# FFN up and gate of a hybrid decoder layer: from feature-major 256-column matmuls to token-major 512-column matmuls, turned back through VectorE and DRAM

## The chip, the cores and the metric

The kernel runs on one core of one Trainium2 chip. A core has a matrix engine (TensorE, PE in the profile, with its weight loads shown as PEld), three engines for elementwise work (VectorE or DVE, ScalarE or ACT, GpSimd or POOL), a queue engine (SyncE, SP) that issues transfers, and 16 DMA engines that carry them. The metric is the device time of one execution in microseconds, given as the median of several runs. Lower is better.

## The reference

The kernel computes one layer of a decoder for 256 tokens of width 1024, all in float32. The first part (norm, two parallel token mixers, an output projection, a residual) is the same before and after. The second part is a gated FFN with a causal convolution over the tokens:

```python
h = rmsnorm(x, norm2_g[l])
up = causal_dwconv(jnp.einsum('bsd,df->bsf', h, w_up[l]), ffn_conv_w[l], ffn_conv_b[l])
act = jax.nn.gelu(up) * jnp.einsum('bsd,df->bsf', h, w_gate[l])
x = x + jnp.einsum('bsf,fd->bsd', act, w_down[l])
```

The FFN is 2816 wide. The convolution has three taps per feature and runs along the tokens, and its weights and bias belong to the feature. A layout with features on the 128 partitions and tokens in the free dimension (feature-major) therefore has one weight per partition, and a tap is a shift in the free dimension. The down projection wants its 128x128 operand with features on the partitions as well.

## The kernel before

**Number format of the matmuls.** Every weight chunk is loaded as float32 (a tile `raw`, 128x2048, 1 MB), split into a rounded part `hi` and a remainder `lo`, and each product is made of three matmuls in TensorE's float32r format (`mm3`, lines 240 to 243: hi by hi, a remainder by hi, hi by the other remainder). The split is one cast on ScalarE (L223; chunks 39, 42 and 43 on VectorE) and one subtraction on VectorE (L224). There are 3 `raw`, 4 `hi` and 3 `lo` buffers.

**The stream of chunks.** All weights form one list, `stream`, in the order of use: chunks 0 to 37 for the first part, 38 to 41 for the output projection, 42 to 74 for the FFN. `advance(i)` emits the splits up to chunk i, and before the split of chunk j the loads up to chunk j+3, all on SP's queue. A load waits until its `raw` buffer has been split; a split waits until TensorE has used the chunk that held its `hi` or `lo` buffer.

**The first part.** The loop over `UNITS` runs the units in the order given; each is cut in quarters. The table `AFTER` names what is emitted behind each quarter: splits (`s5` is the split of chunk 5), evacuations, convolution, recurrence, attention steps (`S`, `P`, `O` with a head's number), and later the four transposes of the second norm (`n00` to `n11`). Two matmul forms occur. `fm_mm` (L245) has a 128x128 block of the weight as the stationary operand and 256 columns, all tokens, as the moving one; its result is feature-major. `tm_mm` (L432) has 128 tokens of the activation as the stationary operand and 512 weight columns as the moving one; its result is token-major, and two tiles hold the two halves of the tokens. With `split=True` the 512 columns come from two blocks of 256 that lie side by side in the chunk; the units ga, gb, pr and pa use this.

**The FFN before.** It has 11 blocks of 256 features. For each block j: up by `fm_mm` (48 matmuls of 256 columns), `up_post` (norm factor `rbf`, convolution, GELU), gate by `fm_mm` (48 more), `gate_post` (multiply, split), and down of block j-1 by `rows_mm` (24 matmuls of 512 columns into the four accumulators `acc`). In block 0 up and gate take the first half of the inner dimension, then the last transposes (`norm2_t(1, 1)`), then the second half; the norm's factors are then broadcast by four matmuls (`norm2_bcast`, tile `rbfp`). The last down block closes the kernel with eight output stores.

**What sets the order.** The framework takes the emitted order as a priority, not as the order itself. A planner walks through the program with its own costs, and puts on each engine's queue the first instruction by priority that it holds to be ready. The order on each queue is then fixed, and on the chip each engine works its queue in that order and waits where data is not there.

Of the kernel before, what the change touches and what calls it, by code (L numbers as in the profile page):

```python
# [8 lines left out]
F32 = mybir.dt.float32  # L9
# [26 lines left out]
AFTER = {  # L36
    "rx0.0": "stats",
    "rg0.0": "s4",
    "rg0.2": "bcast evac1 s5",
    "rg0.3": "s6",  # L40
    "rg1.1": "evac0 evac2",
    "rg1.2": "evac3",
    "rg1.3": "conv0 decay",
    "rg2.0": "s7",
    "rg2.2": "conv1",
    "rg2.3": "s8 split0",
    "k0.1": "s9",
    "k0.2": "s10",
    "k0.3": "conv2 s11",
    "k1.0": "conv3 split1",  # L50
    "k1.3": "s12",
    "k2.3": "s13",
    "ri0.1": "s14",
    "ri0.2": "krs",
    "q0.0": "gelu1",
    "q0.1": "la0 lb0",
    "q0.2": "s15",
    "q1.0": "lc0",
    "q1.2": "s16",
    "q1.3": "s17",  # L60
    "ri1.0": "s18",
    "ri1.3": "ld0 la1",
    "q2.2": "lb1",
    "q3.1": "Tq0 ks0",
    "q3.2": "s19 ks1",
    "q3.3": "s20 qrs gelu0",
    "v0.2": "Tk0",
    "v0.3": "s21",
    "v2.0": "S0",
    "v2.1": "s22",  # L70
    "v2.2": "s23",
    "v3.1": "Tk1",
    "v3.3": "S1 S2",
    "ga0.2": "s24 P0",
    "ga0.3": "s25 lc1 s26 S3",
    "ga1.1": "P1 O0",
    "ga1.3": "Tq1",
    "ga2.1": "P2",
    "ga2.3": "P3",
    "ga3.0": "s27",  # L80
    "ga3.1": "O1",
    "ga3.2": "S6",
    "ga3.3": "S7 O3",
    "gb0.0": "O2 ya0 S4",
    "gb0.1": "S5",
    "gb0.2": "s28",
    "gb1.0": "P6",
    "gb1.2": "ld1 ya1 s29",
    "gb1.3": "P4",
    "gb2.0": "sa1",  # L90
    "gb2.1": "P7 O4",
    "gb2.2": "s30",
    "gb2.3": "ys1",
    "gb3.1": "ys0",
    "gb3.2": "P5",
    "gb3.3": "O6",
    "pr0.0": "s31 sb0",
    "pr0.1": "s32 O5",
    "pr0.2": "O7",
    "pr0.3": "s33",  # L100
    "pr1.2": "sa0",
    "pr2.2": "s34",
    "pr3.2": "s35",
    "pa0.0": "s36",
    "pa1.0": "s37",
    "pa1.3": "s38",
    "pa2.1": "s39",
    "pa2.3": "sb1",
    "pa3.2": "m0",
    "pa3.3": "m1 s40",  # L110
    "wo.3": "m3 s41",
    "wo.5": "m2",
    "wo.11": "n00",
    "wo.12": "s42 n10",
    "wo.15": "n01 s43",
# [4 lines left out]
def trunk_layer(ctx: ExitStack, tc: tile.TileContext, xT, x, vec, win_fm, win_tm, wri, wpr, wpa,  # L120
# [6 lines left out]
    work = ctx.enter_context(tc.tile_pool(name="work", bufs=2))  # L127
    psA = ctx.enter_context(tc.tile_pool(name="psA", bufs=4, space=PSUM))
# [46 lines left out]
    def add(src):  # L175
        stream.append(src)
        return len(stream) - 1
# [560 lines left out]
    act = {}  # L738

    def up_post(j, ps):  # L740
# [3 lines left out]
        for i in range(2):  # L744
            m = 2 * j + i
            w = lambda k: pv[:, V_FW + 3 * m + k:V_FW + 3 * m + k + 1]
            nc.scalar.activation(c[:, i, :], u[:, i, :], AF.Identity, scale=w(2),  # L747
                                 bias=pv[:, V_FB + m:V_FB + m + 1])
            for k in (1, 0):
                d = 2 - k  # L750
                nc.vector.scalar_tensor_tensor(c[:, i, d:], u[:, i, :S - d], w(k), c[:, i, d:],  # L751
                                               op0=OP.mult, op1=OP.add)
# [119 lines left out]
```

## Time and profile before

| | |
|---|---|
| median of three runs | 448.86 us (447.87 to 449.06) |
| the profiled execution | 447.88 us |
| its span, first to last instruction | 446.0 us |
| TensorE busy | 440.8 us, 99% |
| VectorE busy | 313.8 us, 70% |
| ScalarE busy | 261.5 us, 59% |
| DMA, HBM read / written | 79.78 MB / 1.05 MB |
| first up matmul, last acc matmul start | 254.5 us, 440.6 us |

In the profile's rows the number after the engine is the line in the kernel. "out<-in" are the tiles that an instruction writes and reads, xN is a count, and what follows "<-" in a wait is what ended it. In rows of groups the two numbers after the first bar are the busy time in us and the mean duration of one in ns. In a table by stage each engine has its busy time and, in brackets, how many instructions ran; the last three columns are the granted TensorE clock, the busy share of the DMA engines, and GB/s. In rows of a timeline the first number is the start and the second the duration, in us. In rows of DMA issues the last two numbers are the KB of one transfer and the median us from issue to landing. A busy TensorE is no TensorE at its peak, since matmuls overlap.

### The profile page before, as it was taken

How to read it: one execution, taken by the hardware profiler on the slowest of the kernel's cores; microseconds unless marked ns; L12 is line 12 of the kernel's file. 1: busy time of each engine (PE TensorE's matmuls, PEld its weight loads, DVE VectorE, ACT ScalarE, POOL GpSimd, SP SyncE). 2: the span in 40 equal slices, each digit the busy share in tenths (PEclk: the TensorE clock that was granted, in tenths of full speed). 3: DMA queues.
4: the chain of work that ended last, by engine and by line, in shares of the span. 5: the costliest groups of instructions: out<-in, count | busy, mean ns of one | idle time of the engine just before them, and what ended most of it. 6: DMA issues, size and time to landing. Idle time of an engine off the chain costs nothing.

```text
span 446.0 us, 6672 instructions
## 1 busy us (share of the span) xinstructions
PE 440.8 (99%) x2736; PEld 397.3 (89%) x2736; DVE 313.8 (70%) x462; ACT 261.5 (59%) x319; POOL 1.6 (0%) x9
## 2 busy tenths in 40 slices
PE   8999999999999999999999999999999999999996
PEld 8999988888888888888888899999999999999995
DVE  4688996979999775755677888575576575575553
ACT  4687757999996799733141656454354454454420
POOL 1000000000000000000000000000000000000000
PEclk9999999999999999999999999999999999999999
DMA  7995554645575455445545356545645645545202
GB/s 226 373 340 215 216 191 147 205 173 158 181 228 167 127 181 188 155 132 196 191 175 179 114 191 248 195 143 190 220 140 190 216 157 185 202 173 190 94 1 94
DMA packets 17629, 81.24 MB, mean 182 GB/s; under 512 B 1728, under 2 KB 4160, under 8 KB 10944
## 3 DMA queue, kind: packets, MB, share of 16 engines
q1 hardware_dynamic: 16880, 80.22, 51.9%
q10 hardware_dynamic: 720, 0.61, 0.5%
q8 instruction: 21, 0.34, 0.3%
q14 instruction: 8, 0.07, 0.0%
HBM read 79.78 MB, written 1.05 MB: 181 GB/s over the span
## 4 chain that ended last, share of the span: by engine, by line
PE 91%; ACT 5%; DMA 2%; issue 0%; DVE 0%; SPq 0%; ACTq 0%
PE gt L241 5%; PE gt L243 5%; PE gt L242 5%; PE up L243 5%; PE up L242 5%; PE up L241 5%; PE acc L241 4%; PE acc L242 4%; PE acc L243 4%; DMA raw<-in_win_fm 2%; PE rg L241 2%; PE rg L242 2%; PE rg L243 2%; PE ga L241 2%; PE gb L241 2%; PE pr L241 2%
## 5 line engine op out<-in xcount | busy, mean ns | idle before, releaser
L223 ACT CAST hi<-raw 128x2048 fp32r<-128x2048 f32 (+3 forms) x88 | 138.1, 1579 | 100.9 <-PE up L242 32.5
L224 DVE TENSOR_TENSOR lo<-raw,hi 128x2048 fp32r<-128x2048 f32 (+3 forms) x92 | 171.1, 1870 | 32.3 <-PE acc L242 14.0
L241 PE MATMUL up<-h2h,hi 128*128 128x256 f32 x176 | 49.9, 284 | 0.0
L241 PE MATMUL gt<-h2h,hi 128*128 128x256 f32 x176 | 49.9, 283 | 0.0
L243 PE MATMUL up<-h2h,lo 128*128 128x256 f32 x176 | 49.8, 283 | 0.0
L243 PE MATMUL gt<-h2h,lo 128*128 128x256 f32 x176 | 49.8, 283 | 0.0
L242 PE MATMUL gt<-h2l,hi 128*128 128x256 f32 x176 | 49.8, 283 | 0.0
L242 PE MATMUL up<-h2l,hi 128*128 128x256 f32 x176 | 49.8, 283 | 0.0
L241 PEld LDWEIGHTS up<-h2h,hi 128*128 128x128 f32 x176 | 33.7, 192 | 0.4
L242 PEld LDWEIGHTS up<-h2l,hi 128*128 128x128 f32 x176 | 33.7, 192 | 0.3
L242 PEld LDWEIGHTS gt<-h2l,hi 128*128 128x128 f32 x176 | 33.8, 192 | 0.0
L241 PEld LDWEIGHTS gt<-h2h,hi 128*128 128x128 f32 x176 | 33.8, 192 | 0.0
L243 PEld LDWEIGHTS gt<-h2h,lo 128*128 128x128 f32 x176 | 33.8, 192 | 0.0
L243 PEld LDWEIGHTS up<-h2h,lo 128*128 128x128 f32 x176 | 33.7, 192 | 0.0
L241 PE MATMUL acc<-hi,fa 128*128 128x512 f32 x86 | 33.6, 391 | 0.0
L242 PE MATMUL acc<-lo,fa 128*128 128x512 f32 x86 | 33.6, 390 | 0.0
L243 PE MATMUL acc<-hi,fa 128*128 128x512 f32 x86 | 33.5, 389 | 0.0
L743 DVE TENSOR_TENSOR fuc<-up,rbf 128x512 f32<-128x512 f32 x11 | 7.6, 691 | 33.2 <-PE up L243 33.2
L243 PEld LDWEIGHTS acc<-hi,fa 128*128 128x128 f32 x86 | 16.1, 188 | 3.5
L751 DVE SCALAR_TENSOR_TENSOR fuc<-fuc,pv 128x255 f32<-128x255 f32 (+1 forms) x44 | 18.6, 479 | 0.8 <-ACT fuc L747 0.7
L241 PEld LDWEIGHTS acc<-hi,fa 128*128 128x128 f32 x86 | 16.2, 188 | 3.1
L242 PEld LDWEIGHTS acc<-lo,fa 128*128 128x128 f32 x86 | 16.2, 188 | 2.9
(220 smaller groups left out, 1011.1 us busy)
## 6 DMA issues: line engine op xcount, KB each, us to landing
raw<-in_win_tm SPq DMA_DIRECT2D x12, 1024.0 KB, 4.8
raw<-in_win_fm SPq DMA_DIRECT2D x11, 1024.0 KB, 5.7
raw<-in_wup SPq DMA_DIRECT2D x11, 1024.0 KB, 4.8
raw<-in_wgate SPq DMA_DIRECT2D x11, 1024.0 KB, 4.8
raw<-in_wdown SPq DMA_DIRECT2D x11, 1024.0 KB, 4.8
raw<-in_wpr SPq DMA_DIRECT2D x4, 1024.0 KB, 4.9
raw<-in_wpa SPq DMA_DIRECT2D x4, 1024.0 KB, 4.9
raw<-in_wout SPq DMA_DIRECT2D x4, 1024.0 KB, 4.8
```

What stands on the lines that cost most here:

```text
L223: (nc.vector.tensor_copy if on_dve else nc.scalar.copy)(hi[i][:, s], raw[i][:, s])
L224: nc.vector.tensor_sub(lo[i][:, s], raw[i][:, s], f(hi[i][:, s]))
L241: nc.tensor.matmul(o, ah, bh, start=start, stop=False, skip_group_check=skip)
L242: nc.tensor.matmul(o, ah, bl, start=False, stop=False, skip_group_check=skip)
L243: nc.tensor.matmul(o, al, bh, start=False, stop=stop, skip_group_check=skip)
L743: nc.vector.tensor_mul(u, ps, rbf2)
L751: nc.vector.scalar_tensor_tensor(c[:, i, d:], u[:, i, :S - d], w(k), c[:, i, d:], op0=OP.mult, op1=OP.add)
```

## The change

Blocks 0 to 9 become five pairs of 512 features. For each pair, up and gate are computed token-major by `tm_mm` with `split=True`: per result two PSUM tiles (one per 128 tokens), 48 matmuls of 512 columns. The results are then brought to feature-major without TensorE:

- `turn`: VectorE transposes the 32x32 blocks of each PSUM tile within itself into an SBUF tile of 128x1024 (two instructions). Four DMAs, one per group of 32 partitions, write the blocks to a DRAM tile (128 KB each, runs of 1 KB), ordered so that each row of DRAM holds what one feature-major partition needs.
- `back`: one DMA reads the DRAM tile into SBUF (512 KB, rows of 4 KB). It is emitted later, by the entries `ur` and `gr` of `AFTER`. All five DMAs are on SP's queue.
- `pair_up` (entries `fu`): norm factor by two multiplies, convolution of four 128-feature groups, one GELU of 1024 columns. `pair_gate` (entries `fg`): two multiplies by the gate, and the split into the operands of down.

The order is now: in pair 0 up and gate alternate by halves of the inner dimension, in the others up is followed by gate; behind pair p from p = 2 on come the down blocks of pair p-2. After the last pair follow down of blocks 6 and 7, the last block (feature-major as before), and the remaining downs. The stream has the same 33 chunks in the new order. `AFTER` is written anew for the first part as well, and now goes through the FFN. The tiles of the FFN are kept in 15 fixed buffers (`KEPT`).

The diff, with the moved entries of `AFTER` ahead of the FFN cut to samples:

```diff
--- before.py
+++ after.py
+KEPT = {"ups": 1, "upd": 2, "gts": 1, "gtd": 2, "u": 1, "c": 2, "ah": 3, "al": 3}
...
-    "rx0.0": "stats",
-    "rg0.0": "s4",
-    "rg0.2": "bcast evac1 s5",
+    "rx0.0": "stats s4",
+    "rg0.1": "bcast",
+    "rg0.2": "s5 evac1",
...
-    "ga2.3": "P3",
-    "ga3.0": "s27",
-    "ga3.1": "O1",
-    "ga3.2": "S6",
+    "ga2.3": "s27",
+    "ga3.1": "P3",
+    "ga3.2": "O1 S5 S6",
     "ga3.3": "S7 O3",
...
-    "wo.11": "n00",
-    "wo.12": "s42 n10",
-    "wo.15": "n01 s43",
+    "wo.11": "n10 s42",
+    "wo.12": "n00",
+    "wo.14": "s43",
+    "up00.0": "n01 s44",
+    "up00.1": "n11",
+    "up00.3": "bcast2",
+    "gt00.0": "s45",
+    "up01.0": "s46",
+    "gt01.0": "s47",
+    "gt01.1": "ur0",
+    "up10.1": "s48",
+    "up10.2": "gr0",
+    "up11.1": "s49",
+    "up11.3": "fu0",
+    "gt10.1": "s50",
+    "gt10.2": "ur1",
+    "gt11.1": "s51 fg0",
+    "up20.1": "s52",
+    "up20.2": "gr1",
+    "up20.3": "fu1",
...
+    "dn4.1": "s68",
+    "dn4.2": "gr4",
+    "dn4.3": "fu4",
+    "dn5.1": "s69",
+    "dn6.1": "s70",
+    "dn6.3": "fg4",
+    "dn7.1": "s71",
+    "last.0": "s72",
+    "last.2": "s73",
+    "dn8.1": "s74",
 }
...
+    dram = ctx.enter_context(tc.tile_pool(name="dram", bufs=4, space=bass.MemoryType.DRAM))
...
-    c_up, c_gt, c_dn = [], [], []
-    for j in range(NF):
-        c_up.append(add(wup[j]))
-        c_gt.append(add(wgate[j]))
-        if j >= 1:
-            c_dn.append(add(wdown[j - 1]))
-    c_dn.append(add(wdown[NF - 1]))
+
+    NP = NF // 2
+    c_up, c_gt, c_dn = {}, {}, []
+    for p in range(NP):
+        for c, kh in ((c_up, 0), (c_gt, 0), (c_up, 1), (c_gt, 1)) if p == 0 else (
+                (c_up, 0), (c_up, 1), (c_gt, 0), (c_gt, 1)):
+            c[p, kh] = add(two(wup if c is c_up else wgate, 0, 2 * p + kh))
+
+        if p >= 2:
+            c_dn += [add(wdown[j]) for j in (2 * p - 4, 2 * p - 3)]
+    c_dn += [add(wdown[j]) for j in range(2 * NP - 4, 2 * NP - 2)]
+    c_up[NP], c_gt[NP] = add(wup[NF - 1]), add(wgate[NF - 1])
+    c_dn += [add(wdown[j]) for j in range(NF - 3, NF)]
...
-        ps = bank("rbfp")
+        ps = psA.tile([P, 512], F32, tag="A", name="rbfp")
...
-    acc = {(t, hf): psA.tile([P, 512], F32, tag="A", name=f"acc{t}{hf}") for t in range(2) for hf in range(2)}
-    act = {}
+    acc, act, kept = {}, {}, {}
+    def keep(name, p, dt=F32):
+        n = p % KEPT[name]
+        if (name, n) not in kept:
+            kept[name, n] = half(f"f{name}{n}", dt)
+        return kept[name, n]
+    def turn(kind, p, ps):
+        src, dst = keep(kind + "s", p), keep(kind + "d", p)
+        mid = dram.tile([P, 1024], F32, tag="turn", name=f"{kind}m{p}")
+        v = src.rearrange("p (j t c b) -> p t c j b", j=4, t=2, c=4)
+        for t in range(2):
+            nc.vector.transpose(v[:, t], ps[t].rearrange("p (c j b) -> p c j b", c=4, j=4))
+        m = mid.rearrange("(j a) (i f) -> i a j f", j=4, i=4)
+        for i in range(4):
+            nc.sync.dma_start(m[i], src[32 * i:32 * i + 32, :].rearrange("p (j f) -> p j f", j=4))
+        def back():
+            nc.sync.dma_start(dst, mid)
+        item[f"{kind[0]}r{p}"] = back
+        return dst.rearrange("p (i t c b) -> p t c i b", i=4, t=2, c=4)
+    tok32 = lambda a, t: a.rearrange("p (c t i b) -> p t c i b", t=2, i=4, b=32)[:, t]
+    def conv3(c, u, m):
+        w = lambda k: pv[:, V_FW + 3 * m + k:V_FW + 3 * m + k + 1]
+        nc.scalar.activation(c, u, AF.Identity, scale=w(2), bias=pv[:, V_FB + m:V_FB + m + 1])
+        for k in (1, 0):
+            d = 2 - k
+            nc.vector.scalar_tensor_tensor(c[:, d:], u[:, :S - d], w(k), c[:, d:], op0=OP.mult, op1=OP.add)
+    turned, gated = {}, {}
+    def pair_up(p):
+        d = turned["up", p]
+        u, c = keep("u", p), keep("c", p)
+        rb = rbf.rearrange("p (t i b) -> p t i b", t=2, i=4)
+        for t in range(2):
+            nc.vector.tensor_mul(tok32(u, t), d[:, t], rb[:, t, None].to_broadcast([P, 4, 4, 32]))
+        for i in range(4):
+            conv3(kt(c)[:, i, :], kt(u)[:, i, :], 4 * p + i)
+        nc.scalar.activation(c, c, AF.Gelu_apprx_tanh)
+        gated[p] = c
+    def pair_gate(p):
+        c, d = gated[p], turned["gt", p]
+        for t in range(2):
+            nc.vector.tensor_mul(tok32(c, t), d[:, t], tok32(c, t))
+        ah, al = keep("ah", p, F32R), keep("al", p, F32R)
+        split2(ah, al, c)
+        for i in range(2):
+            act[2 * p + i] = tuple(kt(a[:, i * 512:(i + 1) * 512]) for a in (ah, al))
...
-    for j in range(NF):
-        pu, pg = fm_ps(f"up{j}"), fm_ps(f"gt{j}")
-        if j == 0:
-
-            advance(c_up[0] + AHEAD_S)
-            for half_k in range(2):
-                ks = range(4 * half_k, 4 * half_k + 4)
-                for ps, i in ((pu, c_up[0]), (pg, c_gt[0])):
-                    fm_mm(ps, i, h2h, h2l, ks, True)
-                    if not half_k and ps is pu:
-                        norm2_t(1, 1)
-            norm2_bcast()
-            gate_post(0, up_post(0, pu), pg)
-        else:
-            advance(c_up[j] + AHEAD_S)
-            fm_mm(pu, c_up[j], h2h, h2l)
-            c = up_post(j, pu)
-            advance(c_gt[j] + AHEAD_S)
-            fm_mm(pg, c_gt[j], h2h, h2l)
-            gate_post(j, c, pg)
-            advance(c_dn[j - 1] + AHEAD_S)
-            for t in range(2):
-                for hf in range(2):
-                    down(j - 1, t, hf)
+    for p in range(NP):
+        item[f"fu{p}"] = lambda p=p: pair_up(p)
+        item[f"fg{p}"] = lambda p=p: pair_gate(p)
+    item["n11"] = lambda: norm2_t(1, 1)
+    item["bcast2"] = norm2_bcast
+
+    def pair_half(kind, p, kh):
+        c = (c_up if kind == "up" else c_gt)[p, kh]
+        if not kh:
+            open_ps[kind, p] = [bank(f"{kind}{p}{t}") for t in range(2)]
+        advance(c)
+        for k4 in range(4):
+            tm_mm(open_ps[kind, p], c, 4 * kh + k4, k4, h2h, h2l, True)
+            if kh and k4 == 3:
+                turned[kind, p] = turn(kind, p, open_ps[kind, p])
+            yield
+
+    def downs(j):
+        advance(c_dn[j])
+        for t in range(2):
+            for hf in range(2):
+                if j == 0:
+                    acc[t, hf] = psA.tile([P, 512], F32, tag="A", name=f"acc{t}{hf}")
+                down(j, t, hf)
+                yield
+
+    def last_block():
+        pu, pg = fm_ps("upl"), fm_ps("gtl")
+        for ps, i in ((pu, c_up[NP]), (pg, c_gt[NP])):
+            advance(i)
+            for j in range(2):
+                for h in range(2):
+                    fm_mm(ps, i, h2h, h2l, range(4 * h, 4 * h + 4), js=(j,))
+                    if j and h:
+                        if ps is pu:
+                            c = up_post(NF - 1, pu)
+                        else:
+                            gate_post(NF - 1, c, pg)
+                    yield
+
+    for p in range(NP):
+        for kind, kh in (("up", 0), ("gt", 0), ("up", 1), ("gt", 1)) if p == 0 else (
+                ("up", 0), ("up", 1), ("gt", 0), ("gt", 1)):
+
+            run(f"{kind}{p}{kh}", pair_half(kind, p, kh))
+        if p >= 2:
+            run(f"dn{2 * p - 4}", downs(2 * p - 4))
+            run(f"dn{2 * p - 3}", downs(2 * p - 3))
+    run(f"dn{2 * NP - 4}", downs(2 * NP - 4))
+    run(f"dn{2 * NP - 3}", downs(2 * NP - 3))
+    run("last", last_block())
+    run(f"dn{NF - 3}", downs(NF - 3))
+    run(f"dn{NF - 2}", downs(NF - 2))
```

More of the change, by code (lines that the diff above doesn't have):

```diff
@@ new lines @@
+    "rg3.1": "s8",
+    "k0.0": "s9",
+    "k0.1": "conv2",
+    "k0.2": "conv3",
+    "k0.3": "split1",
+    "k1.0": "s10",
+    "k1.3": "s11",
+    "k2.1": "s12",
+    "k2.2": "s13",
+    "k3.1": "s14 gelu1",
+    "ri0.2": "krs",
+    "ri0.3": "s15",
+    "q0.1": "la0 s16 lb0",
+    "q1.1": "s17",
+    "q1.3": "lc0",
+    "ri1.0": "s18",
+    "q2.0": "ld0",
+    "q2.1": "s19",
+    "q2.2": "la1",
+    "q3.0": "lb1 Tq0",
+    "q3.1": "ks0",
+    "q3.2": "gelu0",
+    "v0.1": "qrs",
+    "v0.3": "s20 Tk0",
@@ L83 @@
     "ga3.3": "S7 O3",
[L84 to L88, printed above, removed]
+    "gb0.1": "S4",
+    "gb0.3": "s28",
+    "gb1.0": "O2",
+    "gb1.2": "ld1 s29",
     "gb1.3": "P4",
[L90 to L93, printed above, removed]
+    "gb2.0": "s30 s31",
+    "gb2.1": "P6 ya0 ya1 O4",
+    "gb2.3": "P5",
+    "gb3.0": "P7",
     "gb3.1": "ys0",
-    "gb3.2": "P5",
-    "gb3.3": "O6",
-    "pr0.0": "s31 sb0",
@@ new lines @@
+    "pr2.0": "sa1 O6",
+    "pr2.2": "O5",
+    "pr3.3": "sb1",
+    "pa0.0": "s35 s36",
+    "pa0.3": "s37",
+    "pa1.0": "s38",
+    "pa2.1": "s39",
+    "pa2.2": "s40 m0",
+    "pa3.3": "m1",
+    "wo.3": "s41",
+    "wo.4": "m2",
+    "wo.6": "m3",
+    "wo.11": "n10 s42",
[9 more added lines that the diff above has]
+    "up10.1": "s48",
@@ new lines @@
+    "up10.2": "gr0",
[7 more added lines that the diff above has]
+    "up20.3": "fu1",
+    "up21.1": "s53",
+    "gt20.1": "s54",
+    "gt20.2": "ur2",
+    "gt20.3": "fg1",
+    "gt21.1": "s55",
+    "dn0.1": "s56",
+    "dn0.2": "gr2",
+    "dn0.3": "fu2",
+    "dn1.1": "s57",
+    "up30.1": "s58",
+    "up30.3": "fg2",
+    "up31.1": "s59",
+    "gt30.1": "s60",
+    "gt30.2": "ur3",
@@ L116 @@
+    "gt31.1": "s61",
+    "dn2.1": "s62",
+    "dn2.2": "gr3",
+    "dn2.3": "fu3",
+    "dn3.1": "s63",
+    "up40.1": "s64",
+    "up40.3": "fg3",
+    "up41.1": "s65",
+    "gt40.1": "s66",
+    "gt40.2": "ur4",
+    "gt41.1": "s67",
+    "dn4.1": "s68",
[8 more added lines that the diff above has]
+    "dn8.1": "s74",
 }
@@ L744, in up_post @@
         for i in range(2):
[L745 to L752, printed above, removed]
+            conv3(c[:, i, :], u[:, i, :], 2 * j + i)
         nc.scalar.activation(c, c, AF.Gelu_apprx_tanh)
```

65 lines of the change are left out of this document (19 added, 46 removed).

## The prediction

> **What bounds the kernel now.** I read the page first, then the stages, then PE's row spacing. The first fence is the page's span, its busy times and its chain of work.
>
> ```profile
> span 446.0 us, 6672 instructions
> ...
> PE 440.8 (99%) x2736; PEld 397.3 (89%) x2736; DVE 313.8 (70%) x462; ACT 261.5 (59%) x319; POOL 1.6 (0%) x9
> ...
> PE 91%; ACT 5%; DMA 2%; issue 0%; DVE 0%; SPq 0%; ACTq 0%
> ```
>
> TensorE is 99% busy and holds 91% of the chain. The waits of TensorE say whether it is ever held up; the busy times by stage say how much the others have left (the FFN starts at 254.5):
>
> ```profile
> PE warm L269 <- DVE ones L265: 1.1, 1, 1.1
> PE rx L243 <- DVE lo L224: 0.2, 1, 0.2
> PE rx L241 <- ACT xgh L321: 0.2, 1, 0.2
> ```
>
> ```profile
> 20.00:40.00 20.00, 20.00 (x169) 20.00 (x169) 15.31 (x29) 14.80 (x17) 0.00 (x0) 1.00 0.91 345
> 254.50:280.00 25.50, 25.50 (x210) 25.24 (x209) 21.80 (x43) 17.55 (x24) 0.00 (x0) 1.00 0.59 206
> 280.00:320.00 40.00, 40.00 (x277) 37.38 (x276) 25.25 (x24) 19.26 (x18) 0.00 (x0) 1.00 0.52 185
> ```
>
> After the start TensorE waits for nothing, at full granted clock (1.00). In the FFN VectorE is 63% busy (25.25 of 40), ScalarE 48%, the DMA engines 0.52 at 185 GB/s; elsewhere (20 to 40) they carried 345 GB/s at 0.91. So only what a matmul costs in TensorE's own line can shorten the FFN. Matmuls overlap (each lasts 0.28 or 0.39 us), so the price of one is the distance of the starts, from the timeline of PE:
>
> ```profile
> 260.78 0.28 PE L241 MATMUL up<-h2h,hi 128*128 128x256 f32 x1
> ...
> 263.66 0.28 PE L241 MATMUL gt<-h2h,hi 128*128 128x256 f32 x1
> ```
>
> ```profile
> 207.81 0.39 PE L241 MATMUL pa<-hi,ybh 128*128 128x512 f32 x1
> ...
> 213.25 0.39 PE L241 MATMUL pa<-hi,ybh 128*128 128x512 f32 x1
> ```
>
> ```profile
> 278.50 0.40 PE L241 MATMUL acc<-hi,fa 128*128 128x512 f32 x1
> ...
> 283.74 0.39 PE L243 MATMUL acc<-hi,fa 128*128 128x512 f32 x1
> ```
>
> ```profile
> 150.20 0.40 PE L241 MATMUL ga<-hi,xgh 128*128 128x512 f32 x1
> ...
> 152.04 0.39 PE L243 MATMUL ga<-hi,xgl 128*128 128x512 f32 x1
> ```
>
> 24 matmuls of 256 columns lie between the first two: 2.88/24 = 0.1200 us each. With 512 columns: pa 5.44/24 = 0.2267, acc 5.24/23 = 0.2278, ga 1.84/8 = 0.2300. pa and ga use the very helper and weight layout (two chunks of 256 side by side) that the change gives to up and gate. Twice the columns cost 1.89 to 1.92 times the distance.
>
> **The change, part by part.** *Pace of up and gate.* Ten of eleven blocks go from 960 matmuls of 256 columns to 480 of 512; the last block, all down matmuls and every transpose on TensorE stay. Before: 960 x 0.1200 = 115.2 us. After: 108.8 at pa's pace, 109.3 at acc's, 110.4 at ga's. I take acc's, the row from the same stage with the same neighbours on VectorE and ScalarE: -5.9 us; the ends are -6.4 and -4.8.
>
> [...]
>
> *VectorE and ScalarE.* The groups that price their work:
>
> ```profile
> L224 DVE TENSOR_TENSOR lo<-raw,hi 128x2048 fp32r<-128x2048 f32 (+3 forms) x92 | 171.1, 1870 | 32.3 <-PE acc L242 14.0 <-ACT hi L223 5.5 <-issue 4.9
> L751 DVE SCALAR_TENSOR_TENSOR fuc<-fuc,pv 128x255 f32<-128x255 f32 (+1 forms) x44 | 18.6, 479 | 0.8 <-ACT fuc L747 0.7
> L743 DVE TENSOR_TENSOR fuc<-up,rbf 128x512 f32<-128x512 f32 x11 | 7.6, 691 | 33.2 <-PE up L243 33.2
> L238 DVE TENSOR_TENSOR xal<-xa,xah 128x1024 fp32r<-128x1024 f32 x2 | 2.4, 1224 | 0.0
> L690 DVE SCALAR_TENSOR_TENSOR h2l<-h2T,pv,h2h 128x128 fp32r<-128x128 f32 x16 | 5.3, 347 | 1.4 <-ACT h2h L689 1.2
> ```
>
> The 32x32 turn is in no trace of before. Its form (512 columns, PSUM to SBUF) is that of L743: 0.69 us taken; below it 0.35 (L690, 128 columns), above it 2.29 (a whole 2048-column split, timeline below). Per pair of blocks VectorE then has 6 splits x 2.29 = 13.7, four turns 2.8, 2+2 multiplies 2.8, eight convolution steps 3.8 and a 1024-column split 1.2: 24.3 of the 32.8 us that 144 matmuls at 0.2278 give, 74%; with turns of 2.29 it is 30.7, still inside. ScalarE keeps its form: splits, the same convolution starts, fewer and longer GELU and cast calls. Cost on the path: nothing, covered by TensorE. If VectorE falls behind, splits come late. How late they may come, from the timeline of VectorE, ScalarE and SP:
>
> ```profile
> 300.92 2.29 DVE L224 TENSOR_TENSOR lo<-raw,hi 128x2048 fp32r<-128x2048 f32 x1 [1.68 <-PE acc L242]
> ```
>
> ```profile
> 303.27 0.33 SPq L213 DMA_DIRECT2D raw<-in_wdown  x1
> ```
>
> ```profile
> 312.54 1.91 ACT L223 CAST hi<-raw 128x2048 fp32r<-128x2048 f32 x1 [0.44 <-PE gt L242]
> ```
>
> The split at 300.92 begins when the chunk three back releases lo, ends at 303.2, and is used two chunks later (2 x 48 x 0.1200 = 11.5, at 312.4): 9.2 us to spare. After the change two chunks are 48 x 0.2278 = 10.9 us, 8.6 to spare.
>
> *Five DMAs per result.* Rows of the DMA issues that resemble them:
>
> ```profile
> raw<-in_wup SPq DMA_DIRECT2D x11, 1024.0 KB, 4.8
> raw<-in_wpr SPq DMA_DIRECT2D x4, 1024.0 KB, 4.9
> ...
> xs<-in_x SPq DMA_DIRECT2D x2, 512.0 KB, 7.3
> ...
> raw<-in_wri SPq DMA_DIRECT2D x2, 512.0 KB, 3.7
> out<-xs SPq DMA_DIRECT2D x8, 128.0 KB, 1.9
> ```
>
> Ten results x (4 x 128 KB out + 512 KB back) = 10.5 MB over some 180 us: 58 GB/s on top of 185 x 186/180 = 191, 249 GB/s, against the 345 seen; DMA share about 0.7. An out is the output store's size (1.9 us), the back load lies between 3.7 and 7.3 (I take 3.7: the 7.3 fell into the start, with the queue full). One round trip: a split in front on VectorE 2.3, two turns 1.4, four issues of 0.33 1.3, landing 1.9, issue 0.3, landing 3.7: 10.9 us, 14.5 with 7.3. The list gives it three chunks in every pair (ur0 behind gt01, fu0 behind up11; gr0 and fg0, and later pairs, likewise): 72 x 0.2278 = 16.4 us. Down trails further (dn0 begins four chunks behind fg0's quarter or more), and behind fg4 stand dn7 and the last block. Weight chunks now come as two 4 KB runs per row, which wpr shows to cost 0.1 us of landing.
>
> *SP's queue.* The outs wait on SP for the turns, the back load for four landings, and weight loads stand behind them: 1.9 us at least, 1.4 + 1.3 + 1.9 = 4.6 with the turns and issues. Fifty DMAs more take 50 x 0.33 = 16.5 us of SP's 180. The load issued at 303.27 lands at 308.1, and its cast comes at 312.54: 4.4 us before even the cast is late. The matmuls of that chunk begin five chunks behind 300.92 (four of 5.76, one of 5.47: at 329.4), some 15 us after that cast ends. Cost: nothing. If that cover went, the casts would be late next, then the lo splits with their 8.6 us.
>
> *Norm and lists.* The last transposes move to behind up00.1, the broadcast of the norm to behind up00.3. Its four matmuls could make TensorE wait up to two quarters, 12 x 0.2278 = 2.7 us, if strictly in place; the planner moves work: here is the hi cast of chunk 42 (and 43), listed behind the matmuls that end at 249.6, where n10's transposes stand.
>
> ```profile
> 241.94 2.35 DVE L223 CAST hi<-raw 128x2048 fp32r<-128x2048 f32 x2
> ```
>
> ```profile
> 249.60 0.60 PE L685 MATMUL h2T<-ident,xs 128*128 128x128 f32 x4
> ```
>
> It ran 7.7 us ahead of its place, so lists are priorities, and I take 0 for both this and the moved entries ahead of the FFN, whose instructions are the same. Ends: -0.4 (all that TensorE waited for behind its warm-up) and +2.7 for the broadcast, and for the entries a late attention step, such as O3 two quarters behind P3: a split in front on each of two engines 2.3 + 1.9 with two short steps of about 0.5, 5.2, less 2.7 of cover, +2.5.
>
> *Sum.* -5.9 + 0 + 0. The profiled execution took 447.88 us for its span of 446.0 and lies 0.98 below the median of three; its span becomes 440.1, its time 442.0, and the median 448.86 becomes 443.0.
>
> **The rivals.**
> *A late entry eats about half.* One place ahead of the FFN or at its start costs 2.5 to 2.7 us: 445.6. For it stands VectorE's row of the 40 slices, at 90% or more in seven of the first thirteen, so that a moved entry finds it full:
>
> ```profile
> DVE  4688996979999775755677888575576575575553
> ```
>
> Against it: behind the warm-up TensorE waited 0.4 us in all, by lists of the same kind.
>
> *No better pace.* If the fixed part went with columns instead of matmuls, 512 columns cost 0.240 and nothing changes: 448.9. Against it stand pa, acc and ga. [...]
> *The round trip comes late, and it is slower.* The planner may put the multiply of a turned result ahead of its place, as it did the cast, and then VectorE, in order, stands waiting for the back load with splits behind it. At its listed place this decides only beyond 16.4 + 8.6 = 25.0 us per trip; the worst sum of the rows, out and back each behind a weight load in flight (2 x 4.8 more, 24.1 us), ends just short. Pulled ahead by several us, it starts at correspondingly shorter trips. Each 0.6 us beyond the point, ten times, takes the gain; 1.2 us gives 443.0 + 12 = 455. [...]
>
> **How the numbers follow.** Clean: 0.62, 443.0, its own range 441.5 (pa's pace, and a run at the lowest time shown, 447.87) to 445. Late entry: 0.12 (445 to 448.5). No better pace: 0.04. Round trip late: 0.22 (450 to 465). 0.3% is 1.3 us, about what a measurement here can tell. Faster: 0.62 + 0.09 = 0.71; same 0.03 + 0.04 = 0.07; slower 0.22. The range takes in half of the last case: 441.5 to 455.
>
> **What would show it.** Right: starts of up and gt 0.227 to 0.230 us apart, 480 of them; about 180 us from the first up to the last acc; no TensorE wait above some tenths; VectorE near 74% there; turns near 0.69 us; DMA share near 0.7. Wrong: TensorE idle before up, gt or acc with VectorE's lo or ScalarE's hi as its releaser, VectorE idle with the back load as its releaser, SP waiting long on the outs with weight loads behind, or new waits before 254 us.

## The result, and the profile after

The changed kernel takes 442.77 us (median; 441.97 to 442.99) where the kernel before takes 448.37 us beside it (447.63 to 449.06): a ratio of 0.9872, 95% interval 0.9849 to 0.9895. It is faster by 5.6 us (1.3%), and 443.0 had been predicted. The profiled execution took 442.97 us.

The page after, its span, busy times and chain of work:

```profile
span 441.2 us, 5822 instructions
...
PE 435.9 (99%) x2256; PEld 373.2 (85%) x2256; DVE 323.9 (73%) x477; ACT 260.6 (59%) x309; POOL 1.6 (0%) x9
...
PE 93%; ACT 5%; DMA 1%; issue 0%; DVE 0%; SPq 0%; ACTq 0%
```

TensorE is as full as before (99%), with 480 fewer matmuls; VectorE alone gained busy time, 10 us. The FFN runs from the first up matmul to the last acc matmul. The timeline of TensorE, first of before, then of after:

```profile
254.53 0.36 PE L241 MATMUL up<-h2h,hi 128*128 128x256 f32 x1
...
440.64 0.39 PE L243 MATMUL acc<-hi,fa 128*128 128x512 f32 x1
```

```profile
255.50 0.39 PE L302 MATMUL up<-hi,h2h 128*128 128x512 f32 x1
...
300.56 0.39 PE L302 MATMUL up<-hi,h2h 128*128 128x512 f32 x1
...
311.21 0.39 PE L304 MATMUL up<-hi,h2l 128*128 128x512 f32 x1
...
435.97 0.39 PE L304 MATMUL acc<-hi,fa 128*128 128x512 f32 x1
```

The stretch fell from 186.11 to 180.47 us, by 5.64: all of the gain. Its distances: 47 lie between 300.56 and 311.21, 10.65/47 = 0.2266 us each. The FFN by busy times (PE, PEld, DVE, ACT, POOL, then granted clock, DMA share, GB/s), once whole and twice in parts:

```profile
255.50:436.10 180.60, 180.56 (x847) 151.04 (x846) 128.51 (x155) 85.28 (x77) 0.00 (x0) 1.00 0.68 229
```

```profile
280.00:320.00 40.00, 40.00 (x178) 33.15 (x177) 27.84 (x30) 19.58 (x18) 0.00 (x0) 1.00 0.83 256
320.00:360.00 40.00, 39.96 (x176) 32.78 (x176) 33.51 (x38) 20.37 (x16) 0.00 (x0) 1.00 0.81 280
```

VectorE is busy for 128.51 of 180.6 us, 71% (70 and 84% in the two parts), ScalarE for 47%, the DMA engines at 0.68, and at 0.8 while pairs are in work. The only wait of a TensorE queue in the FFN that comes from the carry's neighbourhood is half a microsecond of its weight loads (two of 0.3 us belong to the second norm). That wait of PEld, then those of SP in the whole kernel (total, times, longest):

```profile
PEld acc L303 <- DVE lo L285: 0.5, 1, 0.5
```

```profile
SPq L820 <- DMA gtm<-fgts: 19.7, 12, 4.8
SPq L820 <- DMA upm<-fups: 18.1, 10, 3.9
```

Line 820 is the load back (817 an out, 814 the turn, 841 the multiply by the norm). SP stood 37.8 us for the landings of ten results, 3.8 us each. What the carry costs, first by the turns of up on VectorE, then by DMA issues (size, median us from issue to landing):

```profile
L814 DVE STREAM_TRANSPOSE fups<-up 128x512 f32<-128x512 f32 x10 | 7.0, 716 | 12.7 <-PE up L304 12.7
```

```profile
upm<-fups SPq DMA_DIRECT2D x20, 128.0 KB, 6.0
...
gtm<-fgts SPq DMA_DIRECT2D x20, 128.0 KB, 7.1
```

A turn is 0.72 us, near the 0.69 taken. An out of 128 KB lands after 6.0 to 7.1 us where the output store of the same size takes 1.9, as before. One whole round trip, up of pair 3, from the timeline of all queues:

```profile
343.93 1.40 DVE L814 STREAM_TRANSPOSE fups<-up 128x512 f32<-128x512 f32 x2 [1.82 <-PE up L304]
...
348.73 0.38 SPq L269 DMA_DIRECT2D raw<-in_wup  x1
...
349.16 2.38 SPq L817 DMA_DIRECT2D upm<-fups  x4
...
356.26 0.34 SPq L820 DMA_DIRECT2D fupd<-upm  x1
...
360.87 1.29 DVE L841 TENSOR_TENSOR fu<-fupd,rbf 128x512 f32<-128x512 f32 x2 [0.37 <-DMA fupd<-upm]
```

The outs leave 5.2 us after the turns began, behind a weight load on SP's queue (348.73); the back load leaves 7.1 us after the first out; the multiply comes 16.9 us after the turn and has waited 0.37 us for its data. TensorE saw none of it: its matmuls have no wait between 255 and 441 us.

### The profile page after: what moved, and what is told of

Same layout as the page of the kernel before. It is cut to its first block, busy times and chain, and to the rows that moved or that the text cites. A ratio compares the mean times of both kernels' runs of the same rounds, so it can differ in the third digit from the quotient of the medians.

```text
span 441.2 us, 5822 instructions
## 1 busy us (share of the span) xinstructions
PE 435.9 (99%) x2256; PEld 373.2 (85%) x2256; DVE 323.9 (73%) x477; ACT 260.6 (59%) x309; POOL 1.6 (0%) x9
## 4 chain that ended last, share of the span: by engine, by line
PE 93%; ACT 5%; DMA 1%; issue 0%; DVE 0%; SPq 0%; ACTq 0%
PE acc L303 4%; PE acc L304 4%; PE acc L302 4%; PE up L304 4%; PE up L302 4%; PE gt L302 4%; PE gt L304 4%; PE gt L303 4%; PE up L303 4%; PE rx L302 2%; PE rx L303 2%; PE rx L304 2%; PE rg L303 2%; PE rg L302 2%; PE rg L304 2%; PE gb L302 2%
## 5 line engine op out<-in xcount | busy, mean ns | idle before, releaser
L285 DVE TENSOR_TENSOR lo<-raw,hi 128x2048 fp32r<-128x2048 f32 (+3 forms) x92 | 170.6, 1866 | 29.6 <-issue 11.4
L303 PE MATMUL acc<-lo,fah 128*128 128x512 f32 x80 | 31.2, 391 | 0.0
L303 PE MATMUL gt<-lo,h2h 128*128 128x512 f32 x80 | 31.2, 390 | 0.0
L303 PE MATMUL up<-lo,h2h 128*128 128x512 f32 x80 | 31.2, 390 | 0.0
L304 PE MATMUL up<-hi,h2l 128*128 128x512 f32 x80 | 31.1, 389 | 0.0
L304 PE MATMUL acc<-hi,fal 128*128 128x512 f32 x80 | 31.1, 389 | 0.0
L302 PE MATMUL up<-hi,h2h 128*128 128x512 f32 x80 | 31.1, 390 | 0.0
L304 PE MATMUL gt<-hi,h2l 128*128 128x512 f32 x80 | 31.0, 389 | 0.0
L302 PE MATMUL acc<-hi,fah 128*128 128x512 f32 x80 | 30.6, 389 | 0.0
L302 PE MATMUL gt<-hi,h2h 128*128 128x512 f32 x80 | 30.5, 389 | 0.0
L302 PE MATMUL rx<-xgh,hi 128*128 128x256 f32 x64 | 18.9, 298 | 0.7 <-ACT xgh L382 0.7
```

What stands on the lines that cost most here:

```text
L285: nc.vector.tensor_sub(lo[i][:, s], raw[i][:, s], f(hi[i][:, s]))
L302: nc.tensor.matmul(o, ah, bh, start=start, stop=False, skip_group_check=skip)
L303: nc.tensor.matmul(o, ah, bl, start=False, stop=False, skip_group_check=skip)
L304: nc.tensor.matmul(o, al, bh, start=False, stop=stop, skip_group_check=skip)
```

## Experiments

The theory was the prediction's: the gain is a fixed part of each matmul (by the rows of before 2 x 0.1200 less 0.2278 us, 12 ns), paid 480 times less, and everything else is covered. The rivals: the gain comes from something else that the change brought (new order, new list, larger weight chunks); or the carry does cost, in part, what the pace gains.

**256 columns in the new order.** The results of a pair are computed with 256 columns per matmul, all else as in the changed kernel.

```diff
-            tm_mm(open_ps[kind, p], c, 4 * kh + k4, k4, h2h, h2l, True)
+            tm_halves(open_ps[kind, p], c, 4 * kh + k4, k4)
+    def tm_halves(ps, i, k, k4):
...
+            for c in range(2):
+                mm3(o[:, c], h2h[k][:, ts], h2l[k][:, ts], at(hi[i])[:, c], at(lo[i])[:, c],
+                    k == 0 and c == 0, k == KT - 1, True)
```

> Everything of the change stays (layout, order, turns, carry), but each matmul of 512 columns in up and gate of the five pairs becomes two of 256 columns with the same stationary operand: 960 instead of 480. Theory (the gain is a fixed part of each matmul, about 12 to 14 ns): starts 0.120 us apart, 960 x 0.120 = 115.2 in place of 109.2, so 442.8 + 6.0 = 448.8, the time of before (448.4) within 0.3%. Rival (the gain comes from the new order and the new lists, not from the column count): 442.8, as after. Second rival (weight loads decide the pace, the same weights loaded twice cost more): above 450.

Measured: 447.83 us, ratio 0.9983 (0.9972 to 0.9995) to the kernel before. Its timeline of TensorE:

```profile
254.77 0.28 PE L302 MATMUL up<-hi,h2h 128*128 128x256 f32 x1
...
295.06 0.28 PE L302 MATMUL gt<-hi,h2h 128*128 128x256 f32 x1
...
299.02 0.28 PE L302 MATMUL gt<-hi,h2h 128*128 128x256 f32 x1
...
441.32 0.39 PE L304 MATMUL acc<-hi,fa 128*128 128x512 f32 x1
```

33 distances in 3.96 us: 0.1200 each, as in before. The FFN takes 186.55 us, 6.08 more than in the changed kernel. By the distances of all starts, up and gate of the five pairs take 115.4 us here and 109.2 in the changed kernel: 6.3 us for the columns per matmul alone. The whole FFN differs by 0.2 us less, because a late split costs the changed kernel 0.34 us and this one half of that. Against before the FFN is 0.44 longer (186.55 less 186.11). Of that, 0.35 are four transposes of the second norm that the new list puts behind the first up matmul instead of ahead of it, and 0.1 lies at the broadcast of the norm. The theory holds; that the order, the list or the larger weight chunks brought the gain falls. Each matmul brings its own weight load (2736 of both here, 2256 in the changed kernel), so the fixed part, 0.2400 less 0.2266 or 13 ns, is that of a matmul with its load; no run separates the two.

**No exchange, no carry.** What is left out: the trip through DRAM and the exchange of blocks among groups of partitions; VectorE turns straight into the tile that the multiplies read.

```diff
-        src, dst = keep(kind + "s", p), keep(kind + "d", p)
-        mid = dram.tile([P, 1024], F32, tag="turn", name=f"{kind}m{p}")
+        dst = keep(kind + "d", p)
...
-        item[f"{kind[0]}r{p}"] = back
+        item[f"{kind[0]}r{p}"] = lambda: None
```

> The carry is left out: VectorE turns the 32x32 blocks straight into the tile that the multiplies read, and the 40 writes and 10 reads of DRAM are gone, so the blocks stand in the wrong places. Theory (the carry is hidden behind TensorE): 442.3 to 442.8, TensorE's wait on a lo split near 328 us (some 0.5 us) gone, landings of the FFN's weights back from 6.0 to 6.5 to about 4.9 us, DMA share of the FFN back to about 0.53. Rival (the carry costs TensorE something that its waits don't show): 439 to 441.

Measured: 441.9 us, ratio 0.9842 (0.9822 to 0.9862). The time lies between the two expectations. The FFN, first up 253.97 to last acc 434.10, takes 180.13 us: 0.34 less than with the carry. All of it lies in the acc matmuls (58.28 us by the distances of their starts, 58.62 in the changed kernel), where the wait of 0.5 us for a split (the late split from here on) is gone. It is not the price of the fifty DMAs and 10.5 MB: two kernels further down keep them, issue them otherwise, and take 180.14 and 180.13 us, without that wait. The order on VectorE differs in all of these kernels. In the changed one it stands 2.77 us ahead of the turn of gate 2 (at 321.84), with a convolution and then the late split behind it. Without the carry the FFN's weights land in 4.8 to 5.6 us instead of 6.0 to 6.5, and the DMA share from 280 to 400 us is 0.57 instead of 0.80.

**The old list ahead of the FFN, twice.** `AFTER` of the kernel before up to and with the output projection, which also puts the four transposes `n01` back ahead of the first up; the new one from there on.

```diff
-    "rx0.0": "stats s4",
-    "rg0.1": "bcast",
+    "rx0.0": "stats",
+    "rg0.0": "s4",
+    "rg0.2": "bcast evac1 s5",
...
```

> The changed kernel, with the entries of the list ahead of the FFN as they were before (n00, n10 and n01 at their old places, n11 and the rest of the FFN as changed). Theory (the moved entries are priorities and cost or gain nothing): 442.8, within 0.3%, and no wait of TensorE above 0.5 us behind its start. Rival (the new list is part of the gain, or costs a part of it): 1.5 to 3 us off in one direction, with TensorE waits ahead of 255 us in one of the two.

Measured: 441.69 us, ratio 0.9837 (0.9821 to 0.9852), about 1 us below the first measurement of the changed kernel. It was therefore measured again beside the changed kernel itself, on one chip.

> The changed kernel itself, once more, beside the next one on the same chip. If the list written anew for the first part costs about 1 us, as 442.77 against the 441.69 of the kernel with the old list would have it, it comes out 0.8 to 1.2 us above that kernel here too. If the profiles are right (from the first rg to the first up 224.83 against 224.86 us, FFN 180.47 against 180.33), it lies within 0.5 us of it, and the difference is the start, which varies by up to 1.5 us between executions.

> The changed kernel with the old list for the part ahead of the FFN, once more, on the same chip as the changed kernel itself. By the profiles (the list moves no time): 0 to 0.5 us from it. By the rival (the new list costs a late entry): 0.8 to 1.2 us below it.

Measured: the changed kernel 441.81 us (441.15 to 442.06; ratio 0.9864, 0.9848 to 0.9881), with the old list 441.63 us (441.2 to 442.89; 0.987, 0.9853 to 0.9886). The list moves nothing that these times can tell. The 1 us between the first measurements lies in the start, as far as the profiles show it. The first rg matmul in the timeline of before, then of after:

```profile
29.67 0.28 PE L241 MATMUL rg<-xgh,hi 128*128 128x256 f32 x1
```

```profile
30.67 0.28 PE L302 MATMUL rg<-xgh,hi 128*128 128x256 f32 x1
```

From there to the first up are 224.86 and 224.83 us. In the second profile of the same changed kernel the first rg comes at 29.78, 0.9 us earlier than in its first.

**A detour: a second DRAM tile in each round trip.** One DMA more per result, from DRAM to DRAM, ahead of the load back.

```diff
         def back():
-            nc.sync.dma_start(dst, mid)
+            mid2 = dram.tile([P, 1024], F32, tag="turn2", name=f"{kind}n{p}")
+            nc.sync.dma_start(mid2, mid)
+            nc.sync.dma_start(dst, mid2)
```

> Each result is copied once more from one DRAM tile to another before it is read back, so that a round trip gets longer by a wait on SP, an issue and a landing, some 5 us: from about 17 us (end of the matmuls to the first multiply, as measured in the changed kernel) to 22 or 23. Theory (a trip may last 25 us, three chunks of 16.4 and 8.6 to spare at the lo splits, before TensorE waits): 442.5 to 444, VectorE waiting several us for the read in some pairs. Rival (the room is used up already, since VectorE waited 1.0 us for the reads): each further us of a trip reaches TensorE, 448 or more.

Measured: 454.03 us, ratio 1.0106 (1.0082 to 1.0131). The theory of ample room falls. The waits of TensorE in the FFN of this kernel, and what ScalarE and VectorE did at the earlier place, from their timelines:

```profile
PE gtl L304 <- DVE lo L285: 2.7, 1, 2.7
PE gt L302 <- ACT hi L284: 2.0, 1, 2.0
PE gt L303 <- DVE lo L285: 1.6, 1, 1.6
```

```profile
311.12 0.72 DVE L814 STREAM_TRANSPOSE fups<-up 128x512 f32<-128x512 f32 x1 [5.68 <-PE up L304]
311.76 3.20 DVE L834 SCALAR_TENSOR_TENSOR fc<-fu,pv,fc 128x255 f32<-128x255 f32 x8
```

```profile
315.04 1.28 ACT L846 ACT_TABLE_LOAD   x1 [7.49 <-DVE fc L834]
...
317.30 1.88 ACT L284 CAST hi<-raw 128x2048 fp32r<-128x2048 f32 x1
```

VectorE waits 5.68 us in order for the next up result, with the convolution behind it; ScalarE waits 7.49 us in order for that convolution, with the hi cast behind it; the cast ends at 319.2, and TensorE has stood for it. From turn to multiply the ten results now take 22 to 35 us (17 to 29 in the changed kernel), yet the loss is not spread over them: it lies at two places, and a second price stands behind each. The granted clock falls: to a mean of 0.88 behind the second (426 to 440 us), and to 0.52 here at the first (columns as in the windows above):

```profile
316.00:320.00 4.00, 1.93 (x8) 0.96 (x6) 2.08 (x3) 3.99 (x4) 0.00 (x0) 1.00 1.04 387
320.00:324.00 4.00, 2.44 (x6) 1.96 (x7) 4.00 (x5) 3.85 (x4) 0.00 (x0) 0.52 0.38 105
```

Added up over the FFN by the distances of the starts, 7.2 us are idle and 4.5 us are matmuls that ran at about half the pace. The late split of the changed kernel (0.34) is gone in return, which leaves the 11.4 us by which the FFN is longer (191.85 against 180.47).

**The detour for gate results alone.**

```diff
+            m2 = mid
+            if kind == "gt":
+                m2 = dram.tile([P, 1024], F32, tag="turn2", name=f"{kind}n{p}")
+                nc.sync.dma_start(m2, mid)
-            nc.sync.dma_start(dst, mid)
+            nc.sync.dma_start(dst, m2)
```

> The detour for the gate results alone (ups come back as in the changed kernel). The first place of the loss (TensorE idle by some 4 us around 316 to 320, then a clock of 0.57) stood behind up 0 and up 1 coming late, the second (gtl's split, 422) lies where SP holds for gate 4. My theory: the first goes, the second stays: 444 to 448, with the FFN stretch 183 to 186. Rival, a loss that goes by the bytes and the holds: half of the 11.4 us, spread over the stretch, 448 with no single wait above 1 us.

Measured: 446.38 us, ratio 0.9952 (0.9934 to 0.997); the FFN takes 184.58 us, 4.1 more than without detour. As the theory had it, the first place is gone and one wait is left. VectorE and TensorE there, from the timelines:

```profile
414.46 0.69 DVE L863 TENSOR_TENSOR fuc<-upl,rbf 128x512 f32<-128x512 f32 x1 [12.78 <-PE upl L304]
415.07 2.28 DVE L285 TENSOR_TENSOR lo<-raw,hi 128x2048 fp32r<-128x2048 f32 x1
```

```profile
417.41 0.38 PE L304 MATMUL gtl<-h2h,lo 128*128 128x256 f32 x1 [2.75 <-DVE lo L285]
...
418.99 0.41 PE L303 MATMUL gtl<-h2l,hi 128*128 128x256 f32 x1
...
420.27 0.41 PE L303 MATMUL gtl<-h2l,hi 128*128 128x256 f32 x1
```

VectorE stood idle for 12.8 us ahead of the norm of the last block, and the split that TensorE needed next stood behind it: a place in a fixed order, not a lack of time. In the changed kernel that same split had run before, at 406.0:

```profile
406.01 2.28 DVE L285 TENSOR_TENSOR lo<-raw,hi 128x2048 fp32r<-128x2048 f32 x1
...
415.65 0.69 DVE L859 TENSOR_TENSOR fuc<-upl,rbf 128x512 f32<-128x512 f32 x1 [6.22 <-PE upl L304]
```

Behind the 2.75 us TensorE's starts lie (420.27 - 418.99)/6 = 0.213 us apart, not 0.120, for some 3.5 us: from 418.50 to 422.00 the granted clock was 0.51, from 422.00 on it was 1.00 again.

**The detour with later entries.** `fu` and `fg` are listed four quarters later. The edit is shown against the kernel with the detour for all results.

```diff
-    "up11.3": "fu0",
+    "gt10.3": "fu0",
-    "gt11.1": "s51 fg0",
+    "gt11.1": "s51",
-    "up20.1": "s52",
+    "up20.1": "s52 fg0",
...
```

> The kernel with the detour through a second DRAM tile (454.03), and the entries fu and fg of the list (from pair 0 on) moved 2 to 4 quarters later, so that VectorE's multiplies stand further behind the loads. My theory: the detour lost its 11 us at two places where an engine in its fixed order stood before a result that was not back, with splits behind it; so the list sets the room, and with later entries most of the loss goes: 442 to 446, without the 2.7 and 2.0 us that TensorE waited at gtl and gt, and the granted clock stays at 1.00. Rival: the detour costs by its traffic and by SP's holds (weights come late), which later entries do not mend: 451 to 455.

Measured: 455.07 us, ratio 1.0161 (1.0116 to 1.0205). My theory that later entries give back the loss falls. The loss moved: 4.0 us now lie ahead of the first down, which waited for the cast of gate 0 (a GELU that ended at 324.2, listed too late for it), and gtl's 2.7 us stayed. Behind this same wait the granted clock stayed at 1.00 here: gtl's 48 distances add up to 8.75 us, against 10.23 in the gate detour and 5.76 in the changed kernel. So the fall of the clock cost 1.5 us there. The rival's number fits, at its upper end; whether SP's holds are the reason was tried next.

**The detour on a queue of its own.** All six DMAs of a result from GpSimd's queue, list as in the detour (the edit against that kernel).

```diff
-            nc.sync.dma_start(m[i], src[32 * i:32 * i + 32, :].rearrange("p (j f) -> p j f", j=4))
+            nc.gpsimd.dma_start(m[i], src[32 * i:32 * i + 32, :].rearrange("p (j f) -> p j f", j=4))
...
-            nc.sync.dma_start(mid2, mid)
-            nc.sync.dma_start(dst, mid2)
+            nc.gpsimd.dma_start(mid2, mid)
+            nc.gpsimd.dma_start(dst, mid2)
```

> The kernel with the detour (454.03), its list as it was, but all six DMAs of a result issued from GpSimd's queue, so that SP carries weight loads only and never waits for a landing of the carry. With the detour on SP, ScalarE waited for weight chunks (8.3 us for the raw of gate in two places, 22.7 us when the entries came later). Theory A: the detour's loss comes by SP's holds, which make weights late, and by the order that the planner draws up around late weights: then the time comes back to 442 to 446 with round trips as long as before (25 us and more). Theory B: the loss comes by the trips themselves, VectorE standing before results that are not back: 450 to 455 still, with TensorE waits of 2 us and more behind VectorE's multiply.

Measured: 456.17 us, ratio 1.018 (1.0163 to 1.0197). Theory A falls: SP carries weights alone, and the loss stays. The traffic of the detour is in all of these runs, and what it adds by itself stays open. TensorE waits at three places, and all three show the prediction's third rival in pure form: VectorE before a result that is not back, and a split behind it. VectorE's timeline, then one of TensorE's waits:

```profile
321.30 1.29 DVE L843 TENSOR_TENSOR fu<-fupd,rbf 128x512 f32<-128x512 f32 x2 [5.99 <-DMA fupd<-upn]
...
356.68 1.29 DVE L852 TENSOR_TENSOR fc<-fgtd,fc 128x512 f32<-128x512 f32 x2 [4.63 <-DMA fgtd<-gtn]
357.89 2.29 DVE L285 TENSOR_TENSOR lo<-raw,hi 128x2048 fp32r<-128x2048 f32 x1
...
412.25 1.29 DVE L843 TENSOR_TENSOR fu<-fupd,rbf 128x512 f32<-128x512 f32 x2 [8.00 <-DMA fupd<-upn]
```

```profile
360.23 0.50 PE L303 MATMUL acc<-lo,fah 128*128 128x512 f32 x1 [3.74 <-DVE lo L285]
```

The turn of the result at 356.68 (gate 2) had begun at 325.85, so the trip took 30.8 us; 3.74 us less would have been free, so that it decides from 27.1 us on. Worked out the same way, the trip decides from 31 us at the first place (up 1: 32.9 us, TensorE waits 1.6) and from 20 us at the third (up 4: 22.7 us, TensorE waits 2.9).

**Why is the trip 17 us?** Two kernels without detour: the five DMAs of a result on GpSimd's queue, and (with the four outs made one) a single write of 512 KB.

```diff
-            nc.sync.dma_start(m[i], src[32 * i:32 * i + 32, :].rearrange("p (j f) -> p j f", j=4))
+            nc.gpsimd.dma_start(m[i], src[32 * i:32 * i + 32, :].rearrange("p (j f) -> p j f", j=4))
...
-            nc.sync.dma_start(dst, mid)
+            nc.gpsimd.dma_start(dst, mid)
```

> The five DMAs of each result are issued from GpSimd's queue instead of SP's; all else is the changed kernel. My theory: the round trip of 17 us (turns of pair 3 at 343.93, multiply at 360.87) is long because the outs stand on SP behind weight loads that wait for a raw buffer and the back load behind four landings (SP waits 19.7 + 18.1 us at line 820 in all); on a queue of their own the outs begin within 1 us of the turns and the trip falls to 10 to 13 us, SP's waits at the back loads vanish; the time does not follow, because TensorE loses only about 0.3 us to the carry: 441.5 to 443, FFN stretch 180.1 to 180.5. Rival A: the landings themselves are slow (6 to 7 us per out, whatever the queue): the trip stays at 15 us or more. Rival B: SP's holds do cost the stream of weights something that is not seen as a wait: the time falls under 441.

```diff
-        m = mid.rearrange("(j a) (i f) -> i a j f", j=4, i=4)
-        for i in range(4):
-            nc.sync.dma_start(m[i], src[32 * i:32 * i + 32, :].rearrange("p (j f) -> p j f", j=4))
+        nc.sync.dma_start(mid, src)
```

> The four writes of each result (32 partitions, runs of 1 KB each) become one write of 128 partitions with rows of 4 KB; the blocks are not put in their places, so the multiply gets wrongly ordered values: the part left out is the exchange of blocks among the partition groups, the bytes and the waits stay. What makes an out land in 6 to 7 us where the output store takes 1.9? Theory: the queue, full of weight chunks: then the single write of 512 KB lands in 5 to 8 us too, and the trip shortens only by the issues (about 1 us). Rival: 32 partitions reach few DMA engines, or runs of 1 KB are slow: then it lands in 3 to 4 us. The time by both: 441.5 to 443, since the trip is covered.

Measured: GpSimd's queue 441.81 us, ratio 0.9872 (0.9857 to 0.9887), FFN 180.14; single write 442.24 us, 0.988 (0.9865 to 0.9894), FFN 180.13. Neither moves the time. The DMA issues of the first, then of the second:

```profile
upm<-fups POOLq DMA_DIRECT2D x20, 128.0 KB, 5.0
...
gtm<-fgts POOLq DMA_DIRECT2D x20, 128.0 KB, 5.5
```

```profile
upm<-fups SPq DMA_DIRECT2D x5, 512.0 KB, 6.5
...
gtm<-fgts SPq DMA_DIRECT2D x5, 512.0 KB, 8.2
```

On a queue of their own the outs still take 5.0 to 5.5 us to land. Up of pair 3 takes 16.6 us from its first turn to its multiply instead of 16.9, but here VectorE works a split between the two turns (VectorE's timeline, then GpSimd's outs):

```profile
342.42 0.72 DVE L814 STREAM_TRANSPOSE fups<-up 128x512 f32<-128x512 f32 x1
...
345.23 0.71 DVE L814 STREAM_TRANSPOSE fups<-up 128x512 f32<-128x512 f32 x1
...
358.98 1.29 DVE L841 TENSOR_TENSOR fu<-fupd,rbf 128x512 f32<-128x512 f32 x2 [2.16 <-DMA fupd<-upm]
```

```profile
346.24 2.34 POOL L817 DMA_DIRECT2D upm<-fups  x4 [14.10 <-DVE fups L814]
```

The outs leave 0.3 us after the second turn, and from its end to the multiply it is 13.0 us, against 15.5 in the changed kernel (345.33 to 360.87). So SP's queue holds 2.5 us of this trip, and my theory is right in that part only; the rest of what the prediction missed is in the landings, as rival A has it. The rival that SP's holds cost TensorE something is worth at most the late split, 0.33 us of the FFN, and the single write, still on SP, does without that too. A single write of 128 partitions lands no sooner (6.5 to 8.2), so neither the 32 partitions nor the 1 KB runs are to blame. What is common to all three is the load of the DMA engines (0.8 while pairs are in work). The 2.5 us above are a wait in SP's order; with GpSimd issuing the outs, their landings still take 5.0 and 5.5 us. That the engines' load is the cause is inferred. The reverse is seen: without the carry the weights land 0.9 to 1.6 us sooner (above). No run took the weights away.

## Why the prediction was right

*Pace of up and gate.* Right in mechanism and size. -5.9 was taken; the run with 256 columns shows -6.3 for it alone by the distances of the starts (-6.08 by the whole FFN). Undisturbed, the distance is 0.2266 us, that of pa rather than the 0.2278 of acc that I had chosen; its end of the range, -6.4, was the nearer row.

*VectorE and ScalarE.* Right: turns 0.72 us for up and 0.71 for gate against 0.69, VectorE at 71% against 74%, no cost on the path.

*Five DMAs per result.* Cost right (nothing; the 0.34 us lost at one split goes when the same DMAs are issued otherwise), sizes wrong. The DMA share came out as said (0.68 against 0.7), the rate below it (229 against 249 GB/s). The mis-sized term is the round trip: 10.9 us taken, 14.5 at the far end, 16.9 measured. An out was priced at 1.9 us by the output store, which runs when the weights are through; among weight loads it takes 6.0 to 7.1. And the outs left 5.2 us after the turns began, behind a weight load, which only the "worst sum" of 24.1 had counted.

*SP's queue.* Right: 3.8 us per result within 1.9 to 4.6, hidden to within the 0.33 us by which the FFN is shorter on GpSimd's queue.

*Norm and lists.* Right to some tenths: 224.83 against 224.86 us ahead of the FFN, and the old list measured beside the new one is no different. But the 0.35 us of the four transposes left the part ahead of the FFN without making it shorter, so a third of a microsecond is lost there, and none had been put down for it. The rival "a late entry eats about half" falls.

*The round trip comes late.* The mechanism was sound, and 25.0 us lies in the middle of the points seen in the detour on GpSimd's queue, 20, 27.1 and 31 at three places; one point for all does not exist. Its price was put wrongly: ten times the excess. The detours show one to three places, not ten, where an order fixed ahead meets a late result, up to 4 us each, and 1.5 to 3 us more where the clock fell. That 454 to 456 is near the 455 of this rival is no proof of its sum. Nor is 25 us the one measure: with the detour on SP, for all results or for the gates alone, the longest single wait was for a split that the fixed order had put behind the norm of the last block, with no late trip directly ahead of it.

*The sum.* -5.9 against -5.64 in the FFN. By the distances of the starts that is -6.2 for all matmuls of up and gate, +0.35 for the four transposes that moved into the stretch, +0.1 for the broadcast and +0.1 for the acc matmuls, the late split (0.34) among them. So the pace was taken 0.3 too small and the three others at nothing, and the errors cancel in part. That the time came out within 0.3 us of 443.0 is luck as well: measured again, the same kernel took 441.81 beside 447.65, a gain of 5.8 us. The chance of 0.22 for a slower kernel was not idle: one DMA more per result takes the whole gain, and nearly as much again.

## What to carry to other kernels

Where TensorE is 99% busy and its waits are nil, count its instructions, price them by the distance of starts in the same trace, and look for the same columns in fewer matmuls (here 0.2266 us for 512 columns against 2 x 0.1200 for 256). A detour through DRAM of 17 to 29 us from turn to multiply left the matmuls without a wait here, since the multiplies stand far enough behind in VectorE's order (0.37 us of waiting at up of pair 3); with 22 to 35 us it cost 11.4. Price its landings by rows among the same traffic (6.0 to 7.1 us for an out, not the 1.9 of the output store), and find the instruction that stands behind the waiting one. When an order is fixed ahead, lengthening a hidden step can cost at places that the step does not touch: in the gate detour TensorE waited 2.75 us for a split behind the norm of the last block.

## What was unexpected in the hardware

- Behind 2.75 us of idle TensorE the granted clock fell to 0.51 for 3.5 us, so that the wait cost about 1.5 times its length (by the starts 2.9 us idle and 1.5 us lost to slow matmuls, gate detour). It does not always fall: with later entries it stayed at 1.00 behind a wait of 2.74 us. Two of the seven runs of the gate detour have a mean clock of 1.000 and the lowest times, 444.71 and 445.24 us, the other five 0.996 and 446.2 to 447.25. What decides is not shown. The windows of the gate detour, then of the run with later entries:

```profile
418.50:422.00 3.50, 3.50 (x20) 3.50 (x19) 3.50 (x5) 2.47 (x3) 0.00 (x0) 0.51 0.76 297
```

```profile
425.00:429.00 4.00, 3.10 (x26) 3.10 (x27) 4.00 (x8) 2.54 (x3) 0.00 (x0) 1.00 0.49 156
```

- The start differs by up to a microsecond between executions of one kernel (first rg at 30.67 and at 29.78 us), more than the whole carry costs; a difference of spans is to be read from a common first instruction.
